# A batched matmul fed from HBM: loads and stores on one queue, and a hardware loop in the middle

## The chip, the cores and the metric

The kernel runs on one core of a Trainium2 chip. The time is device microseconds of that core; the kernel before has a median of 531.79 us over 14 runs (530.21 to 534.66). The profile is of one execution, which took 531.62 us, and from its first to its last instruction it spans 529.5 us.

## The reference

There are 8 x 16 = 128 independent products of a 256 x 512 matrix with a 512 x 384 matrix, in float32:

```python
b1, b2, m, k, n = 8, 16, 256, 512, 384
x = randn(b1, b2, m, k);  weight = randn(b1, b2, k, n)      # float32
out = np.matmul(x, weight)                                   # (8, 16, 256, 384) float32
```

The inputs are 67.1 MB of x and 100.7 MB of weight, the output is 50.3 MB: 218.1 MB cross HBM once.

## The kernel before, in words

The batch is worked off in pairs of products. For a pair, x comes in as one tile of 128 partitions by 2048 numbers (1 MB, `load_x`, L60), and each of the two weights as one tile of 128 by 1536 (768 KB, `load_w`, L67). VectorE casts the x tile to bfloat16 (L77), TensorE transposes it in sixteen 128 x 128 pieces into PSUM (L82), VectorE copies those back to SBUF (L86), and VectorE casts the two weights (L110). TensorE then multiplies: 32 matmuls for a pair (L124), each with 64 columns of stationary x and 384 columns of weight, the two products of the pair side by side in the two halves of PSUM's partitions. ScalarE copies each of the two PSUM tiles to SBUF (L131), and one DMA of 768 KB stores the pair's result (L95). The last pair is taken as two groups of one product each (`groups`, L41), with full 128-column matmuls and two stores of 384 KB.

All loads are issued from SP, all stores from ACT; these are two DMA queues. The whole batch is unrolled: each engine has one straight list of instructions. The order within an engine's list is made by the framework's scheduler from the order of the program. `LAG = 3` (L43) asks for stores three groups late; in the built program each store nevertheless stands on ACT right behind the two copies of its own pair. Tiles come from pools, which reuse buffers in turn: 3 x tiles, 6 float32 weight tiles, so three pairs of loads can be in SBUF; 6 output tiles. Besides the wait for a free buffer, a DMA waits for the DMA eight places before it on the semaphore that both share: there are eight such semaphores, over both queues together, so about eight transfers, two pairs' worth of loads and stores, are in flight.

Of the kernel before, what the change touches and what calls it, by code (L numbers as in the profile page):

```python
# [1 line left out]

# [5 lines left out]


@with_exitstack
def kernel(
    ctx: ExitStack,
    tc: tile.TileContext,
    x: bass.AP,
    weight: bass.AP,
    out: bass.AP,
):
    nc = tc.nc
    P = 128  # L20

    b1, b2, M, K = x.shape
    _, _, _, N = weight.shape
    B = b1 * b2
    KO = K // P

    x_rows = x.rearrange("b1 b2 m k -> (b1 b2 m) k")
    o_rows = out.rearrange("b1 b2 m n -> (b1 b2 m) n")
    w_flat = weight.rearrange("b1 b2 k n -> (b1 b2) k n")

    fp32 = mybir.dt.float32
    bf16 = mybir.dt.bfloat16

    GX = 2
    CX = P // GX
    R = GX * M // P


    groups = [2] * ((B - GX) // 2) + [1] * GX  # L41

    LAG = 3  # L43

    const = ctx.enter_context(tc.tile_pool(name="const", bufs=1))
    x_pool = ctx.enter_context(tc.tile_pool(name="x_pool", bufs=3))
    xb_pool = ctx.enter_context(tc.tile_pool(name="xb_pool", bufs=2))
    xt_pool = ctx.enter_context(tc.tile_pool(name="xt_pool", bufs=2))
    w_pool = ctx.enter_context(tc.tile_pool(name="w_pool", bufs=6))
    wb_pool = ctx.enter_context(tc.tile_pool(name="wb_pool", bufs=4))  # L50
    out_pool = ctx.enter_context(tc.tile_pool(name="out_pool", bufs=LAG + 3))
    psum_t = ctx.enter_context(tc.tile_pool(name="psum_t", bufs=2, space=bass.MemoryType.PSUM))
    psum_o = ctx.enter_context(tc.tile_pool(name="psum_o", bufs=3, space=bass.MemoryType.PSUM))

    identity = const.tile([P, P], bf16)
    make_identity(nc, identity)

    def load_x(b):
        x_sb = x_pool.tile([P, R, K], fp32, name="x_sb")
        nc.sync.dma_start(  # L60
            x_sb[:], x_rows[b * M : (b + GX) * M].rearrange("(p r) k -> p r k", r=R)
        )
        return x_sb

    def load_w(b):
        w_sb = w_pool.tile([P, KO, N], fp32, name="w_sb")
        nc.sync.dma_start(w_sb[:], w_flat[b].rearrange("(kp ko) n -> kp ko n", ko=KO))  # L67
        return w_sb

    def transpose_x(x_sb, RG):  # L70


        H = R // RG
        x_bf = xb_pool.tile([P, R, K], bf16, name="x_bf")
        x_t = xt_pool.tile([P, RG, KO, P, H], bf16, name="x_t")
        for r0 in range(0, R, 4):
            nc.vector.tensor_copy(out=x_bf[:, r0 : r0 + 4], in_=x_sb[:, r0 : r0 + 4])  # L77
            for r in range(r0, r0 + 4, 2):
                pt = psum_t.tile([P, 2, KO, P], bf16, name="pt")
                for rr in range(2):  # L80
                    for ko in range(KO):
                        nc.tensor.transpose(  # L82
                            pt[:, rr, ko, :], x_bf[:, r + rr, ko::KO], identity
                        )
                j = r % RG
                nc.vector.tensor_copy(  # L86
                    out=x_t[:, j : j + 2, :, :, r // RG], in_=pt[:]
                )
        return x_t

    waiting = []

    def store():
        dram, out_sb = waiting.pop(0)
        nc.scalar.dma_start(out=dram, in_=out_sb)  # L95

    b = 0
    for n, G in enumerate(groups):
        last = n == len(groups) - 1
        C = P // G  # L100
        RG = G * M // P
        if b % GX == 0:
            x_sb = load_x(b)
        w_sb = [load_w(b + i) for i in range(G)]
        if b % GX == 0:
            x_t = transpose_x(x_sb, RG)
        w_bf = []
        for i in range(G):
            t = wb_pool.tile([P, KO, N], bf16, name="w_bf")
            nc.vector.tensor_copy(out=t[:], in_=w_sb[i][:])  # L110
            w_bf.append(t)
        if last:
            while waiting:
                store()

        out_full = out_pool.tile([P, 2 * M // P, N], fp32, name="out_sb")
        out_sb = out_full[:, :RG]
        for r in range(0, RG, 2):
            po = psum_o.tile([P, 2, 512], fp32, name="po")
            for rr in range(2):  # L120
                for ko in range(KO):
                    for i in range(G):
                        c0 = (b % GX + i) * CX
                        nc.tensor.matmul(  # L124
                            po[i * C : (i + 1) * C, rr, :N],
                            x_t[:, r + rr, ko, c0 : c0 + CX, :],
                            w_bf[i][:, ko, :],
                            start=(ko == 0),
                            stop=(ko == KO - 1),
                        )  # L130
            nc.scalar.copy(out=out_sb[:, r : r + 2, :], in_=po[:, :, :N])  # L131
        waiting.append(
            (
                o_rows[b * M : (b + G) * M].rearrange("(p r) n -> p r n", r=RG),
                out_sb,
            )
        )
        if len(waiting) > LAG or last:
            store()
        b += G  # L140


# [1 line left out]
_INS = ['x', 'weight']  # L144
_OUTS = [((8, 16, 256, 384), 'float32')]


# [23 lines left out]
```

## Time and profile before

| | before |
|---|---|
| median of 14 runs | 531.79 us |
| the profiled execution, its time | 531.62 us |
| its span, first to last instruction | 529.5 us |
| TensorE matmuls, busy | 344.1 us (65%) |
| VectorE, busy | 277.8 us (52%) |
| ScalarE, busy | 103.8 us (20%) |
| DMA queue of the loads: bytes, share of the 16 DMA engines | 167.78 MB, 76.3% |
| DMA queue of the stores | 50.34 MB, 22.9% |
| instruction fetch of one engine's list: packets, bytes | 24, 0.39 MB |
| mean granted TensorE clock | 0.857 |

Times on the page are microseconds unless marked ns. "PE" is TensorE, "PEld" its weight loads, "DVE" VectorE, "ACT" ScalarE, "SPq" and "ACTq" the instruction sequencers that issue DMAs. A share of DMA near 1.00 in a stretch means that all 16 DMA engines had a packet under way all the time; it can pass 1 a little, since records of successive packets overlap by a few ns. In a row of groups, what stands behind the second bar is the engine's idle time just before those instructions and what ended it. L numbers are lines of the kernel.

### The profile page before, as it was taken

The page shows a single profiled execution, that of the slowest core. Times are in us where ns is not written, and L with a number is a line of the kernel's source. Part 1 is how long each engine was busy: PE and PEld are TensorE (multiplying, and loading weights), DVE is VectorE, ACT ScalarE, POOL GpSimd, SP SyncE. Part 2 cuts the span into 40 slices and gives each one's busy share as a digit, 9 for nine tenths or more (in the row PEclk, how much of TensorE's full clock was granted, in tenths as well). Part 3 has the DMA queues.
Part 4 walks back from the last instruction along what each step waited for, and adds up shares of the span by engine and source line. Part 5 has one row for each costly group of instructions (what it writes and reads, how often), then busy time and mean ns, then how long its engine had stood idle before and what let it go on. Part 6 is the DMA issues. An engine that isn't in the chain of part 4 may idle for free.

```text
span 529.5 us, 7363 instructions
## 1 busy us (share of the span) xinstructions
PE 344.1 (65%) x3056; PEld 235.0 (44%) x3056; DVE 277.8 (52%) x320; ACT 103.8 (20%) x129; POOL 0.7 (0%) x6
## 2 busy tenths in 40 slices
PE   4576674675765857646758567576585685765854
PEld 2354453453543535434435345354353454543532
DVE  4555555545546454655554554554645645465454
ACT  1221221211212212112122121121121211212212
POOL 0000000000000000000000000000000000000000
PEclk9988789979788796898697986978979869689798
DMA  8999999999999999999999999999999999999994
GB/s 346 398 424 422 425 420 422 426 419 421 425 420 424 420 422 425 421 423 423 420 424 423 421 422 423 422 423 424 420 422 423 421 424 422 421 422 424 420 401 166
DMA packets 37041, 218.59 MB, mean 413 GB/s; under 512 B 4112, under 2 KB 4112, under 8 KB 28816
## 3 DMA queue, kind: packets, MB, share of 16 engines
q1 hardware_dynamic: 27648, 167.78, 76.3%
q10 hardware_dynamic: 9360, 50.34, 22.9%
q8 instruction: 24, 0.39, 0.3%
q14 instruction: 9, 0.07, 0.0%
HBM read 167.77 MB, written 50.33 MB: 412 GB/s over the span
## 4 chain that ended last, share of the span: by engine, by line
DMA 83%; PE 9%; DVE 5%; issue 1%; SPq 1%; DVEq 0%; ACT 0%
DMA w_sb<-in_weight_dram 46%; DMA x_sb<-in_x_dram 37%; PE po L124 8%; DVE w_bf L110 3%; DVE x_t L86 2%; PE pt L82 1%; SPq L67 0%; DVEq L166 0%; DVE x_bf L77 0%; SPq L60 0%; ACT out_sb L131 0%; DVEq L110 0%; DVEq L77 0%
## 5 line engine op out<-in xcount | busy, mean ns | idle before, releaser
L124 PE MATMUL po<-w_bf,x_t 128*64 128x384 bf16 (+1 forms) x2032 | 276.5, 407 | 165.8 <-DVE w_bf L110 165.0
L124 PEld LDWEIGHTS <-x_t 128*64 128x64 bf16 (+1 forms) x2032 | 174.6, 135 | 252.3 <-DVE w_bf L110 126.7
L131 ACT COPY out_sb<-po 128x768 f32<-128x768 f32 x128 | 102.6, 801 | 421.6 <-PE po L124 421.6
L77 DVE CAST x_bf<-x_sb 128x2048 bf16<-128x2048 f32 x64 | 78.5, 1227 | 135.7 <-DMA x_sb<-in_x_dram 135.7
L110 DVE CAST w_bf<-w_sb 128x1536 bf16<-128x1536 f32 x128 | 119.8, 954 | 28.4 <-DMA w_sb<-in_weight_dram 27.6
L86 DVE COPY x_t<-pt 128x1024 bf16<-128x1024 bf16 x128 | 83.6, 695 | 81.5 <-PE pt L82 81.5
L82 PE MATMUL pt<-identity,x_bf 128*128 128x128 bf16 x1024 | 70.5, 223 | 15.4 <-DVE x_bf L77 15.2
L82 PEld LDWEIGHTS <-x_bf 128*128 128x128 bf16 x1024 | 60.4, 115 | 37.6 <-DVE x_bf L77 28.9
L131 ACT ACT_TABLE_LOAD x1 | 1.3, 1283 | 0.7 <-PEq L155 0.7
masks.py:199 POOL TENSOR_SCALAR_AFFINE_SELECT identity<-identity 128x128 bf16<-128x128 bf16 x1 | 0.3, 294 | 0.1
masks.py:197 POOL MEMSET identity<- 128x128 bf16 x1 | 0.2, 206 | 0.3 <-POOLq L155 0.3
L155 POOL MEMSET const-bfloat16-1.0<- 128x1 bf16 x1 | 0.1, 102 | 0.0
L155 POOL MEMSET const-uint8-127<- 128x1 uint8 x1 | 0.1, 102 | 0.0
L155 POOL MEMSET const-float32-0.0<- 128x1 f32 x1 | 0.1, 99 | 0.2 <-issue 0.2
L155 POOL MEMSET const-float32-1.0<- 128x1 f32 x1 | 0.1, 99 | 0.0
## 6 DMA issues: line engine op xcount, KB each, us to landing
w_sb<-in_weight_dram SPq DMA_DIRECT2D x128, 768.0 KB, 16.1
x_sb<-in_x_dram SPq DMA_DIRECT2D x64, 1024.0 KB, 16.0
out_dram<-out_sb ACTq DMA_DIRECT2D x63, 768.0 KB, 8.3
out_dram<-out_sb ACTq DMA_DIRECT2D x2, 384.0 KB, 2.3
```

The source lines that it names most:

```text
L77: nc.vector.tensor_copy(out=x_bf[:, r0 : r0 + 4], in_=x_sb[:, r0 : r0 + 4])
L82: nc.tensor.transpose(pt[:, rr, ko, :], x_bf[:, r + rr, ko::KO], identity)
L86: nc.vector.tensor_copy(out=x_t[:, j : j + 2, :, :, r // RG], in_=pt[:])
L110: nc.vector.tensor_copy(out=t[:], in_=w_sb[i][:])
L124: nc.tensor.matmul(po[i * C : (i + 1) * C, rr, :N], x_t[:, r + rr, ko, c0 : c0 + CX, :], w_bf[i][:, ko, :], start=(ko == 0), stop=(ko == K ...
L131: nc.scalar.copy(out=out_sb[:, r : r + 2, :], in_=po[:, :, :N])
L155: nc = _bacc.Bacc("TRN2", target_bir_lowering=False, num_devices=1)
```

## The change

Four things are done together.

1. The stores move from ACT to SP, and SP issues everything in the order in which the program says it: for pair s the two weight loads, the x load, and then the store of pair s-4. The weights now come before x, except in the last pair, where x still comes first and the four stores still owed follow its loads.
2. Buffers are persistent and named, not taken from pools: 4 x tiles, 8 float32 weight tiles and 8 output tiles (four pairs of loads, eight pairs of results); two PSUM tiles for results in place of three, four for transposes in place of two.
3. The first eight pairs and the last eight stay unrolled. The 48 between run in a hardware loop of six iterations with eight pairs each. The loads' and stores' addresses are worked out in registers, and the waits inside compare semaphores with counts in registers, so that no barrier stands between iterations.
4. The built program shows what happens at the loop's ends. Nothing waits on the way in. At the exit SP waits until every DMA of the loop has landed and VectorE, ScalarE and TensorE have finished the loop's last pair; then all engines meet at a barrier, and only then SP issues the next load. The stores of the loop's last four pairs are issued after the exit, each behind the loads of a later pair.

What each engine computes is unchanged: the same casts, transposes, matmuls and copies, in nearly the same order.

```diff
-    groups = [2] * ((B - GX) // 2) + [1] * GX
-    LAG = 3
+    U = 8
+    LAG = 4
...
-    x_pool = ctx.enter_context(tc.tile_pool(name="x_pool", bufs=3))
-    w_pool = ctx.enter_context(tc.tile_pool(name="w_pool", bufs=6))
-    out_pool = ctx.enter_context(tc.tile_pool(name="out_pool", bufs=LAG + 3))
-    psum_t = ctx.enter_context(tc.tile_pool(name="psum_t", bufs=2, space=bass.MemoryType.PSUM))
-    psum_o = ctx.enter_context(tc.tile_pool(name="psum_o", bufs=3, space=bass.MemoryType.PSUM))
+    x_sb = [pool.tile([P, R, K], fp32, name=f"x_sb{s}") for s in range(4)]
+    w_sb = [pool.tile([P, KO, N], fp32, name=f"w_sb{s}") for s in range(8)]
+    w_bf = [pool.tile([P, KO, N], bf16, name=f"w_bf{s}") for s in range(4)]
+    out_sb = [pool.tile([P, R, N], fp32, name=f"out_sb{s}") for s in range(8)]
+    pt = [psum.tile([P, 2, KO, P], bf16, name=f"pt{s}") for s in range(4)]
+    po = [psum.tile([P, 2, 512], fp32, name=f"po{s}") for s in range(2)]
...
-    def store():
-        dram, out_sb = waiting.pop(0)
-        nc.scalar.dma_start(out=dram, in_=out_sb)
+    def store(b, s, g=G):
+        nc.sync.dma_start(
+            out=o_rows[bass.ds(b * M, g * M)].rearrange("(p r) n -> p r n", r=g * M // P),
+            in_=out_sb[s % 8][:, : g * M // P],
+        )
...
+    def pair(b, s, lagged):
+        load_w(b, 2 * s)
+        load_w(b + 1, 2 * s + 1)
+        load_x(b, s)
+        for i in range(G):
+            cast_w(2 * s + i)
+        product(transpose_x(s, R), G, 0, [2 * s, 2 * s + 1], s, 0)
+        if lagged:
+            store(b - G * LAG, s - LAG)
+
+    for s in range(U):
+        pair(G * s, s, s >= LAG)
+    with tc.For_i(G * U, B - G * U, G * U, iteration_sync="reg_based") as b:
+        for s in range(U):
+            pair(b + G * s, U + s, True)
+    b = B - G * U
+    for s in range(U - 1):
+        pair(b + G * s, s, True)
+
+    s = U - 1
+    b += G * s
+    load_x(b, s)
+    load_w(b, 2 * s)
+    load_w(b + 1, 2 * s + 1)
+    for k in range(LAG, 0, -1):
+        store(b - G * k, s - k)
+    xt = transpose_x(s, M // P)
+    for i in range(G):
+        cast_w(2 * s + i)
+        product(xt, 1, i, [2 * s + i], s + i, i)
+        store(b + i, s + i, 1)
```

More of the change, by code (lines that the diff above doesn't have):

```diff
@@ L27 @@
     x_rows = x.rearrange("b1 b2 m k -> (b1 b2 m) k")
+    w_rows = weight.rearrange("b1 b2 k n -> (b1 b2 k) n")
     o_rows = out.rearrange("b1 b2 m n -> (b1 b2 m) n")
-    w_flat = weight.rearrange("b1 b2 k n -> (b1 b2) k n")
     fp32 = mybir.dt.float32
     bf16 = mybir.dt.bfloat16
-    GX = 2
-    CX = P // GX
-    R = GX * M // P
-    groups = [2] * ((B - GX) // 2) + [1] * GX
-    LAG = 3
-    const = ctx.enter_context(tc.tile_pool(name="const", bufs=1))
-    x_pool = ctx.enter_context(tc.tile_pool(name="x_pool", bufs=3))
@@ L47 @@
-    xb_pool = ctx.enter_context(tc.tile_pool(name="xb_pool", bufs=2))
-    xt_pool = ctx.enter_context(tc.tile_pool(name="xt_pool", bufs=2))
-    w_pool = ctx.enter_context(tc.tile_pool(name="w_pool", bufs=6))
-    wb_pool = ctx.enter_context(tc.tile_pool(name="wb_pool", bufs=4))
-    out_pool = ctx.enter_context(tc.tile_pool(name="out_pool", bufs=LAG + 3))
-    psum_t = ctx.enter_context(tc.tile_pool(name="psum_t", bufs=2, space=bass.MemoryType.PSUM))
-    psum_o = ctx.enter_context(tc.tile_pool(name="psum_o", bufs=3, space=bass.MemoryType.PSUM))
@@ L55 @@
-    identity = const.tile([P, P], bf16)
-    make_identity(nc, identity)
-    def load_x(b):
-        x_sb = x_pool.tile([P, R, K], fp32, name="x_sb")
+    G = 2
+    C = P // G
+    R = G * M // P
+    PAIRS = B // G
+    U = 8
+    LAG = 4
+    pool = ctx.enter_context(tc.tile_pool(name="sb", bufs=1))
+    psum = ctx.enter_context(tc.tile_pool(name="ps", bufs=1, space=bass.MemoryType.PSUM))
+    identity = pool.tile([P, P], bf16, name="identity")
+    make_identity(nc, identity)
+    x_sb = [pool.tile([P, R, K], fp32, name=f"x_sb{s}") for s in range(4)]
@@ new lines @@
+    x_bf = [pool.tile([P, R, K], bf16, name=f"x_bf{s}") for s in range(2)]
+    x_t = [pool.tile([P, R, KO, P], bf16, name=f"x_t{s}") for s in range(2)]
+    w_sb = [pool.tile([P, KO, N], fp32, name=f"w_sb{s}") for s in range(8)]
[3 more added lines that the diff above has]
+    po = [psum.tile([P, 2, 512], fp32, name=f"po{s}") for s in range(2)]
@@ L60, in load_x @@
+    def load_x(b, s):
         nc.sync.dma_start(
-            x_sb[:], x_rows[b * M : (b + GX) * M].rearrange("(p r) k -> p r k", r=R)
-        )
[L63 to L70, printed above, removed]
-        H = R // RG
[L74 to L89, printed above, removed]
@@ L91 @@
-    waiting = []
-    def store():
-        dram, out_sb = waiting.pop(0)
[L95 to L119, printed above, removed]
+            x_sb[s % 4][:],
@@ new lines, in load_x, with load_w, transpose_x @@
+            x_rows[bass.ds(b * M, G * M)].rearrange("(p r) k -> p r k", r=R),
+        )
+    def load_w(b, s):
+        nc.sync.dma_start(
+            w_sb[s % 8][:],
+            w_rows[bass.ds(b * K, K)].rearrange("(p ko) n -> p ko n", ko=KO),
+        )
+    def store(b, s, g=G):
+        nc.sync.dma_start(
+            out=o_rows[bass.ds(b * M, g * M)].rearrange("(p r) n -> p r n", r=g * M // P),
+            in_=out_sb[s % 8][:, : g * M // P],
+        )
+    def transpose_x(s, RG):
+        H = R // RG
+        xt = x_t[s % 2].rearrange("k r ko c -> k (r ko c)").rearrange(
+            "k (j ko c h) -> k j ko c h", j=RG, ko=KO, c=P, h=H
+        )
+        nc.vector.tensor_copy(out=x_bf[s % 2][:], in_=x_sb[s % 4][:])
+        for r in range(0, R, 2):
+            t = pt[(2 * s + r // 2) % 4]
@@ L120, with cast_w @@
             for rr in range(2):
                 for ko in range(KO):
-                    for i in range(G):
-                        c0 = (b % GX + i) * CX
+                    nc.tensor.transpose(
+                        t[:, rr, ko, :], x_bf[s % 2][:, r + rr, ko::KO], identity
+                    )
+            j = r % RG
+            nc.vector.tensor_copy(out=xt[:, j : j + 2, :, :, r // RG], in_=t[:])
+        return xt
+    def cast_w(s):
+        nc.vector.tensor_copy(out=w_bf[s % 4][:], in_=w_sb[s % 8][:])
@@ L124, with product @@
+    def product(xt, g, i0, ws, o, n):
+        RG = g * M // P
+        for r in range(0, RG, 2):
+            p = po[(n + r // 2) % 2]
+            for rr in range(2):
+                for ko in range(KO):
+                    for i in range(g):
+                        rows = slice(i * (P // g), (i + 1) * (P // g))
                         nc.tensor.matmul(
-                            po[i * C : (i + 1) * C, rr, :N],
-                            x_t[:, r + rr, ko, c0 : c0 + CX, :],
-                            w_bf[i][:, ko, :],
+                            p[rows, rr, :N],
+                            xt[:, r + rr, ko, (i0 + i) * C : (i0 + i + 1) * C, :],
+                            w_bf[ws[i] % 4][:, ko, :],
@@ L130 @@
                         )
[L131 to L140, printed above, removed]
+            nc.scalar.copy(out=out_sb[o % 8][:, r : r + 2, :], in_=p[:, :, :N])
+    def pair(b, s, lagged):
[27 more added lines that the diff above has]
+        store(b + i, s + i, 1)
 _INS = ['x', 'weight']
```

## The prediction

> **What bounds the kernel now.** I read the page's DMA part first, then the busy time of stretches, then the DMA queue's own waits, then the end in order of time. From the page:
>
> ```profile
> PE 344.1 (65%) x3056; PEld 235.0 (44%) x3056; DVE 277.8 (52%) x320; ACT 103.8 (20%) x129; POOL 0.7 (0%) x6
> ...
> q1 hardware_dynamic: 27648, 167.78, 76.3%
> q10 hardware_dynamic: 9360, 50.34, 22.9%
> q8 instruction: 24, 0.39, 0.3%
> ...
> DMA 83%; PE 9%; DVE 5%; issue 1%; SPq 1%; DVEq 0%; ACT 0%
> ```
>
> The two queues take 76.3 + 22.9 = 99.2% of sixteen DMA engines; the busiest compute engine stands at 65%. The stretches (columns: PE, weight loads, DVE, ACT, POOL with counts, then clock, DMA share, GB/s) say when:
>
> ```profile
> 0.00:2.00 2.00, 0.00 (x0) 0.00 (x0) 0.00 (x0) 1.27 (x1) 0.70 (x6) 1.00 0.27 33
> 2.00:4.00 2.00, 0.00 (x0) 0.00 (x0) 0.00 (x0) 0.01 (x1) 0.00 (x0) 1.00 0.74 295
> ...
> 300.00:320.00 20.00, 12.62 (x108) 8.55 (x110) 10.05 (x12) 3.20 (x4) 0.00 (x0) 0.82 1.02 422
> ...
> 514.00:516.00 2.00, 1.85 (x14) 1.40 (x15) 0.09 (x1) 0.00 (x0) 0.00 (x0) 0.57 0.70 295
> 516.00:518.00 2.00, 2.00 (x18) 1.54 (x15) 0.77 (x1) 0.80 (x1) 0.00 (x0) 0.57 0.60 250
> 518.00:520.00 2.00, 1.60 (x22) 1.09 (x18) 1.26 (x2) 0.80 (x1) 0.00 (x0) 1.00 0.22 88
> ...
> 526.00:528.00 2.00, 0.00 (x0) 0.00 (x0) 0.00 (x0) 0.17 (x1) 0.00 (x0) 0.98 0.84 335
> ```
>
> From 4 to 514 us the DMA engines are full, at 421 to 423 GB/s in every stretch of 20 us between 40 and 500. Only the ends have slack. What SP waits for is not data but a place:
>
> ```profile
> SPq L67 <- DMA w_sb<-in_weight_dram: 255.0, 123, 4.0
> SPq L60 <- DMA x_sb<-in_x_dram: 172.3, 61, 4.6
> ```
>
> That is 427 us of waiting for earlier transfers to land (one of the eight in flight), and about 6 us for VectorE (3.0 + 2.9). So loads are always queued ahead. The end, in order of time:
>
> ```profile
> 517.23 1.23 DVE L77 CAST x_bf<-x_sb 128x2048 bf16<-128x2048 f32 x1 [3.13 <-DMA x_sb<-in_x_dram]
> ...
> 521.56 1.81 DVE L110 CAST w_bf<-w_sb 128x1536 bf16<-128x1536 f32 x2
> 522.55 2.39 PEld L124 LDWEIGHTS <-x_t 128*128 128x128 bf16 x16 [3.11 <-DVE w_bf L110]
> ...
> 524.89 0.34 ACTq L95 DMA_DIRECT2D out_dram<-out_sb  x1
> ...
> 526.20 0.34 ACTq L95 DMA_DIRECT2D out_dram<-out_sb  x1
> ```
>
> The share falls to 0.70, 0.60, 0.22 while loads are still landing: some of the 16 engines have finished and others are late (the last weight packet ends near 520.5). From 514 on, with 353, 46 and 54 GB/s in the stretches left out and 5 in the last, 2 x (295+250+88+353+46+54+335+5) KB = 2.85 MB move in 15.5 us, where 6.8 us would do: 8.7 us are idle.
>
> [...] both queues together make 99.2%, and the loads-only stretch from 4 to 16 us runs at 415 to 441 GB/s, as the mixed ones do. [...]
>
> **The change, part by part.**
>
> *Stores on SP, one order: 0 in the middle.* An issue costs SP 0.33 us; four per pair are 1.3 us of the 3.41 MB / 422 = 8.1 us that a pair takes. The address arithmetic and the register waits come on top; the trace has none, so I bound them by nothing and by another 0.5 us each, 3.3 us per pair, still under 8.1. Behind a store on SP stand the next pair's loads. The store of pair s-4 waits for ScalarE; that pair's loads landed two pairs (16 us) before, and landing to second copy takes some 9 us, so it finds its data ready. If not, 13 us of queued transfers cover it.
>
> *Deeper buffers, weights first: 0.* The limit is eight in flight, and it stays. TensorE's and VectorE's work per pair (344.1/64 = 5.4 and 277.8/64 = 4.3 us) fits in 8.1.
>
> *Back-edges: 0, five of them.* TensorE's loop body is some 796 instructions, three blocks; its packets may be fetched anew in each iteration, and a stall of one packet's length (about 1 us) or several is covered by 2.7 us of slack per pair on TensorE and 13 us of queue on SP. Without that cover it would be 5 x 1 to 4 = 5 to 20 us. Extra fetches load the DMA engines: some 6 more packets of 1 to 1.4 us over 16 engines, 0.5 us.
>
> *End: a gain.* Five pairs' stores (3.93 MB, 9.3 us) remain behind the last loads, where before it was two. They cover the last pair's compute, which from the last weight landing takes about 4 us up to the last store's issue (0.96 cast, half of 2.77 matmul, 0.80 copy, waits). So the end is DMA-bound.
>
> *Exit: the loss.* The DMA engines empty once. In the loop's last pair x lands last, at T, with one store behind it in the queue (0.786 MB, 1.9 us). Durations are from the timeline near 305 us: landing to cast 0.5; cast 1.23; wait and transposes until the first copy 0.7; copy 0.65; 32 matmuls 3.3 (full clock) to 5.5, I take 4.2; last copy with wait 0.9. ScalarE ends at T + 8.2. Barrier: 0.6, estimated from the 1.3 us between the last store packet (near 528.2) and the span's end, which hold a landing and more than one barrier. SP's first issue at 0.74 has its first packet near 2.4: 1.65. Packets flow at T + 10.45, after 8.5 us of idleness. Bounds: 6.5 (full clock, no barrier cost, copy overlapped) and 11 (low clock, and a fetch when the loop branch falls through).
>
> *The sum, on the span.* Start: 2(1-33/422) + 2(1-295/422) = 2.4. A dip at 16 to 20 us (364 and 298 GB/s): 0.9, kept. Up to the exit 56 pairs of loads (2.621 MB each) and 52 stores: 187.7 MB / 422.3 = 444.4. The slowest engine is late at the exit: before, the end loses (1-0.70)+(1-0.60)+(1-0.22), times 2, = 3.0 us to this over the whole run; I take 2. Exit 8.5. After it 30.4 MB / 422.3 = 72.0, slowest engine 1.5. Last packet to span end 1.3, fetches 0.5. Total 2.4 + 0.9 + 444.4 + 2 + 8.5 + 72.0 + 1.5 + 1.3 + 0.5 = 533.5, against 529.5. The profiled execution took 2.1 more than its span, and the median lies 0.2 above it: 533.5 + 2.3 = 535.8, I say 536.0, slower by 0.8%.
>
> **Rivals.** 0.2% (1.06 us) is about what a measurement of this kernel can tell from no change.
>
> *Uneven engines and fetches go away; ends faster.* If the loop's instructions stay in place, fetches fall from 24 packets to about 9 and the engines stay level. That removes the 2 + 1.5 of lateness, the 0.5, and 15 x 1.4/16 = 1.3, in all 5.3: 528.2 + 2.3 = 530.5. It decides only from 5.3 us on, since 536.0 - 530.7 must be made up. For it: [...] packets of instructions stand between data packets. [...] 0.11.
>
> *Exit and end cancel: no change.* Exit at 6.5 and half of the lateness gone: 536.0 - 2.0 - 1.8 = 532.2. 0.11.
>
> *The loop's own cost shows.* Back-edges or SP's register work leave fewer than eight in flight, or the exit takes 11 with a late fetch. Five edges at 1 us and exit 11: 536.0 + 5 + 2.5 = 543.5. Against: 13 us of queue. 0.12.
>
> *Forecast: 536.0*, own range 533 to 539. 0.66.
>
> **How the numbers follow.** The likeliest gives 536.0. The range takes in the no-change case, the exit's upper bound and part of the loop's cost: 531.3 to 542, leaving out the faster case and the worst edges. Faster 0.11; same 0.09 (most of the cancelling case); slower 0.80.
>
> **What would show it.** DMA share 1.0 at 422 GB/s through the loop and across back-edges; one hole of about 8 us near 450 us, with ScalarE's last copy and a barrier in it; a tail without the 8.7 us of idleness, last loads landing near 522; SP's waits still on landed transfers, not on ScalarE. Wrong, if holes recur every eight pairs (65 us), if the hole is under 5 or over 11 us, or if the rate inside the loop is not 422.

## The result, and the profile after

The changed kernel takes 542.21 us (median of 10 runs, 541.2 to 543.62), against 531.82 us for the kernel before in the same comparison: 1.0186 times as long, with a 95% interval of 1.0166 to 1.0206. The forecast was 536.0, with a range up to 542.0. The direction was right, the size was not: 10.4 us were lost where some 4 were foreseen.

The profiled execution took 542.08 us and spans 540.3. Its page, whose second line is the mean rate in 40 slices of 13.5 us:

```profile
DMA  8999699999999999999999999999999995799998
GB/s 352 418 410 421 250 379 424 423 423 422 425 423 424 425 423 424 422 424 424 423 423 424 424 424 424 425 424 423 424 424 424 425 424 233 234 425 423 421 424 329
...
q1 hardware_dynamic: 37008, 218.12, 97.6%
q8 instruction: 9, 0.15, 0.1%
```

All data now go through one queue. In the loop, from slice seven on, the rate is 422 to 425 GB/s, and no stretch of 20 us between 80 and 440 us, back-edges among them, is under 422. There are two holes, not one: slice five (54 to 68 us), where the loop begins, and slices 34 and 35 (446 to 473 us), where it ends. And the instruction packets of q8 are 9, where they were 24. In the packet records, which list every transfer with its start and size, each has 16384 bytes, one comes at 113 us and the next at 463. I take them for TensorE's: its 2 x 3056 matmuls and weight loads share the 24 packets at some 64 bytes each, and the page counts no more than 320 instructions on any other engine.

The hole at the loop's start, in stretches of 2 us (last two columns: share of the DMA engines, GB/s):

```profile
58.00:60.00 2.00, 1.30 (x16) 0.67 (x12) 0.96 (x1) 1.46 (x2) 0.00 (x0) 1.00 0.83 345
60.00:62.00 2.00, 0.00 (x0) 0.00 (x0) 1.07 (x1) 0.14 (x1) 0.00 (x0) 1.00 0.15 62
62.00:64.00 2.00, 1.45 (x20) 1.18 (x22) 1.27 (x3) 0.00 (x0) 0.00 (x0) 0.98 0.05 11
64.00:66.00 2.00, 2.00 (x16) 1.15 (x14) 0.17 (x1) 0.00 (x0) 0.00 (x0) 0.50 0.72 230
66.00:68.00 2.00, 2.00 (x18) 1.09 (x14) 0.00 (x0) 0.80 (x1) 0.00 (x0) 0.67 0.71 227
```

and at its end:

```profile
452.00:454.00 2.00, 0.00 (x0) 0.00 (x0) 0.57 (x1) 0.79 (x1) 0.00 (x0) 1.00 0.56 236
454.00:456.00 2.00, 1.08 (x16) 0.93 (x16) 1.24 (x2) 0.00 (x0) 0.00 (x0) 1.00 0.05 22
...
460.00:462.00 2.00, 0.64 (x8) 0.21 (x4) 0.00 (x0) 0.80 (x1) 0.00 (x0) 1.00 0.00 0
462.00:464.00 2.00, 0.00 (x0) 0.00 (x0) 0.00 (x0) 0.00 (x0) 0.00 (x0) 0.82 0.41 91
```

I price a hole as the bytes that 424 GB/s would have moved more: each stretch of 2 us at r GB/s loses 2 (1 - r/424). From 58 to 74 us that gives 7.2 us, from 452 to 466 us 10.5, and from 468 to 472, where 247 and 287 GB/s flow though the DMA engines are busy (shares of 1.04 and 0.91), 1.5 more. The same sum is used for every kernel below.

What SP waited for between 44 and 72 us:

```profile
SPq L67 <- DVEq L130: 14.8, 1, 14.8
SPq L73 <- ACTq L130: 2.3, 1, 2.3
```

L130 is the line of the loop. SP's first load of the loop waited 14.8 us for VectorE's sequencer, and its first store 2.3 us for ScalarE's, each to come to the loop itself. The instructions in order of time show it (start, duration):

```profile
46.70 0.34 SPq L73 DMA_DIRECT2D out_dram<-out_sb  x1
...
60.92 1.23 DVE L85 CAST x_bf<-x_sb 128x2048 bf16<-128x2048 f32 x1 [1.50 <-DMA x_sb<-in_x_dram]
...
62.88 1.29 DVE L94 COPY x_t<-pt 128x1024 bf16<-128x1024 bf16 x2 [0.73 <-PE pt L90]
63.51 1.61 SPq L67 DMA_DIRECT2D w_sb<-in_weight_dram  x2
...
68.17 0.80 ACT L116 COPY out_sb<-po 128x768 f32<-128x768 f32 x1 [1.16 <-PE po L109]
68.33 0.36 SPq L73 DMA_DIRECT2D out_dram<-out_sb  x1
```

SP has issued everything ahead of the loop by 47 us, two pairs before VectorE. Its next issue comes at 63.51, when VectorE has begun the last copy of pair 7, the last pair before the loop. Meanwhile the two pairs in flight land, and at 60 us the transfers stand idle. The first store follows ScalarE's last copy of pair 7 in the same way.

The reason stands in the built program. Inside the loop SP compares counters (semaphores) that belong to the loop, one for each engine, with counts in registers. The program has each engine give its own counter a starting value as the last thing before it enters the loop, so until VectorE has got there the load waits, although the last cast from the buffer that it wants, one of pair 4's, had ended by 35.02 us. The instruction records show it: SP's wait on VectorE's counter begins at 48.65 us, VectorE raises that counter at 63.35 and branches into the loop at 63.71, and the wait ends at 63.40; the wait on ScalarE's counter begins at 65.93, ScalarE raises it at 68.18, and the wait ends at 68.22. "Nothing waits on the way in", as I described the change above, is wrong.

The exit:

```profile
453.43 1.23 DVE L85 CAST x_bf<-x_sb 128x2048 bf16<-128x2048 f32 x1 [1.49 <-DMA x_sb<-in_x_dram]
...
460.80 0.80 ACT L116 COPY out_sb<-po 128x768 f32<-128x768 f32 x1 [1.08 <-PE po L109]
462.22 0.82 SPq L67 DMA_DIRECT2D w_sb<-in_weight_dram  x2
```

This is the chain of the forecast: 8.2 us from the start of the cast to the end of ScalarE's last copy (461.60), where I had 7.7; and 0.62 us from there to SP's first issue, the barrier, where I had 0.6.

### The profile page after: what moved, and what is told of

Its sections match the earlier page's. It is cut to its first block, busy times and chain, and to the rows that moved or that the text cites. A ratio compares the mean times of both kernels' runs of the same rounds, so it can differ in the third digit from the quotient of the medians.

```text
span 540.3 us, 8649 instructions
## 1 busy us (share of the span) xinstructions
PE 322.0 (60%) x3056; PEld 211.7 (39%) x3056; DVE 285.0 (53%) x320; ACT 103.6 (19%) x129; POOL 0.7 (0%) x6
## 5 line engine op out<-in xcount | busy, mean ns | idle before, releaser
L109 PE MATMUL po<-w_bf,x_t 128*64 128x384 bf16 (+1 forms) x2032 | 235.7, 398 | 17.2 <-DVE x_t L94 14.0
L90 PE MATMUL pt<-identity,x_bf 128*128 128x128 bf16 x1024 | 87.8, 252 | 196.8 <-DVE x_bf L85 196.8
L109 PEld LDWEIGHTS <-x_t 128*64 128x64 bf16 (+1 forms) x2032 | 136.9, 134 | 103.8 <-DVE x_t L94 22.6
L98 DVE CAST w_bf<-w_sb 128x1536 bf16<-128x1536 f32 x128 | 122.4, 958 | 88.6 <-DMA w_sb<-in_weight_dram 82.8
L90 PEld LDWEIGHTS <-x_bf 128*128 128x128 bf16 x1024 | 74.8, 125 | 220.1 <-DVE x_bf L85 219.8
L94 DVE COPY x_t<-pt 128x1024 bf16<-128x1024 bf16 x128 | 86.0, 697 | 61.5 <-PE pt L90 42.2
```

The source lines that it names most:

```text
L90: nc.tensor.transpose(t[:, rr, ko, :], x_bf[s % 2][:, r + rr, ko::KO], identity)
L94: nc.vector.tensor_copy(out=xt[:, j : j + 2, :, :, r // RG], in_=t[:])
L98: nc.vector.tensor_copy(out=w_bf[s % 4][:], in_=w_sb[s % 8][:])
L109: nc.tensor.matmul(p[rows, rr, :N], xt[:, r + rr, ko, (i0 + i) * C : (i0 + i + 1) * C, :], w_bf[ws[i] % 4][:, ko, :], start=(ko == 0), sto ...
```

## The experiments

Two theories of the loss. **Ends:** the loop costs time at its two ends alone, at the entry because SP waits for the engines behind it to enter, at the exit because SP waits for the last pair's compute and a barrier. **Order or fixed prices:** the one queue and its order cost the time, or going in and out of a loop stops the engines for a fixed time of its own. In what follows "the changed kernel" is the one above, with its single loop.

### The loop written out

```diff
-    with tc.For_i(G * U, B - G * U, G * U, iteration_sync="reg_based") as b:
+    for b in range(G * U, B - G * U, G * U):
         for s in range(U):
             pair(b + G * s, U + s, True)
```

> The changed kernel with its hardware loop written out: the same order on SP, the same lag of four, the same named buffers, one straight list per engine. Theory (the loop's two ends cost the time: 7.2 us lost near 60 us at the entry, about 12 us near 455 us at the exit): both holes vanish, the rate falls back from 424 to 422 GB/s since TensorE's instructions are fetched all the way again, and the later stores fill the end: span about 526, median about 528, that is 0.7% faster than the kernel before. Rival (the one queue or the order of weights before x costs the time, the loop's ends only show it): slower than the kernel before, 535 or more, with holes that recur.

Measured: 525.75 us, 0.9882 (0.9842 to 0.9922) of the kernel before. Both holes are gone; the same stretches as above:

```profile
58.00:66.00 8.00, 3.79 (x40) 2.33 (x36) 4.44 (x5) 1.02 (x2) 0.00 (x0) 0.87 1.02 423
452.00:464.00 12.00, 7.57 (x77) 4.85 (x78) 7.09 (x9) 2.36 (x3) 0.00 (x0) 0.86 1.02 426
```

The one queue, the order and the buffers are no loss: without the loop they are 1.2% faster than before, and 2 us faster than I expected. The loop alone costs 542.21 - 525.75 = 16.5 us. The holes at its ends are 7.2 + 10.5 + 1.5 = 19.2 us. Two things give some of it back. From 100 to 440 us, by the packet records, data move at 423.8 GB/s in the loop and at 422.3 in the written-out kernel, which is 1.4 us over the 163.6 MB of the 48 pairs; the instruction packets' own bytes are 0.9 of these 1.5 GB/s, and what the rest comes from was not tried. And the end loses 3.0 us (from 520 us on) where the written-out kernel's loses 4.4 (from 504 on). That leaves 19.2 - 1.4 - 1.4 = 16.4, all but 0.1 of the difference.

### The stores back on ACT, without the loop

```diff
-        nc.sync.dma_start(
+        nc.scalar.dma_start(
             out=o_rows[bass.ds(b * M, g * M)].rearrange("(p r) n -> p r n", r=g * M // P),
```

on top of the written-out kernel. The scheduler puts each store right behind its own pair's copies again.

> The changed kernel without its loop, and with the stores back on ACT, each behind the two copies of its own pair. It tells what the one queue and the lag of four are worth alone. Theory (the lag keeps stores for the end, where the transfers stand idle otherwise): about 531.5, as the kernel before, some 3 us above the unrolled one with stores on SP. Rival (the queue that a store is issued on makes no difference, since a transfer waits its turn either way): equal to the unrolled one within 1 us.

Measured: 531.66 us, 0.9993 (0.9979 to 1.0007): the kernel before. So the order of weights and x, four pairs of buffers in place of three, and the division of PSUM are worth nothing together, and the 5.9 us (I had expected some 3) come from the stores. Where, the last stretches say; first this kernel, then the written-out one with stores on SP:

```profile
518.00:520.00 2.00, 2.00 (x28) 1.25 (x23) 1.42 (x2) 0.93 (x2) 0.00 (x0) 1.00 0.22 85
520.00:522.00 2.00, 0.84 (x16) 0.68 (x13) 1.57 (x2) 0.68 (x1) 0.00 (x0) 1.00 0.27 111
522.00:524.00 2.00, 1.04 (x7) 0.66 (x8) 1.74 (x2) 0.00 (x0) 0.00 (x0) 1.00 0.73 295
524.00:526.00 2.00, 1.73 (x11) 0.83 (x9) 0.00 (x0) 1.03 (x2) 0.00 (x0) 1.00 0.00 0
```

```profile
514.00:516.00 2.00, 0.00 (x0) 0.00 (x0) 2.00 (x3) 0.00 (x0) 0.00 (x0) 1.00 0.99 401
516.00:518.00 2.00, 1.51 (x10) 0.93 (x11) 1.30 (x2) 0.00 (x0) 0.00 (x0) 1.00 0.65 270
518.00:520.00 2.00, 1.26 (x8) 0.55 (x6) 0.00 (x0) 1.45 (x2) 0.00 (x0) 1.00 0.55 224
520.00:522.00 2.00, 0.00 (x0) 0.00 (x0) 0.00 (x0) 0.14 (x1) 0.00 (x0) 0.83 0.86 344
```

While the last pair is computed, the first has little or nothing to move, and the second moves the stores kept back. From 510 us on this kernel loses 9.3 us, and the one with stores on SP 4.4 from 504 on: 4.9 us of the difference. The rest is in the middle: from 100 to 440 us data move at 421.3 GB/s here and in the kernel before, and at 422.3 with the stores on SP, which is 1.2 us over 218.1 MB. Whether that small part comes from the queue or from where the stores stand was not tried.

### Stores two and six groups behind, without the loop

```diff
-    LAG = 4
+    LAG = 2
```

and the same with 6.

> The loop written out, stores two groups behind their loads in place of four. Theory (each store kept back for the end is worth its 1.86 us of transfer there): three stores behind the last loads in place of five, 525.75 + 3.7 = 529.5, unless SP's wait for ScalarE lets the queue run dry in the middle, then more. Rival (the gain came from the one queue): 526 within 1 us.

> The loop written out, stores six groups behind. Theory: two more stores at the end, of which only what is idle there can be filled: from 512 us on the unrolled kernel loses about 4.6 us, some 2 of it after the last transfer, so 523 to 524. Rival (the end is bound by the last pair's compute alone): 525.75 within 0.5 us.

Measured: 530.26 (0.9971, 0.9957 to 0.9985) and 525.13 us (0.9883, 0.9858 to 0.9908). With two it is 4.5 us above the lag of four, where two stores' transfers are 3.7, and all of this on the one queue: it is mainly the stores kept for the end that count, not the queue. SP then waits 344.5 us in total for ScalarE, in front of each store, yet the rate in the middle holds (no stretch of 2 us between 30 and 470 us is under 400 GB/s): SP's waits are hidden there behind the transfers that are queued. Six brought 0.6 us by the medians, not the 2 that I expected, and nothing by the ratios to the kernel before, which are 0.9883 and 0.9882. From 514 us on the rates are 392, 332, 272 and 151 GB/s, at DMA shares of 0.95, 0.80, 0.66 and 0.38: I read this as some of the 16 engines having finished their share and others not, and more stores did not mend it. Lags of four and six are the fastest kernels of this study.

### Loads two pairs ahead, with the loop

```diff
-    def pair(b, s, lagged):
-        load_w(b, 2 * s)
-        load_w(b + 1, 2 * s + 1)
-        load_x(b, s)
+    AHEAD = 2
+
+    def pair(b, s, lagged, ahead=True):
+        if ahead:
+            loads(b + G * AHEAD, s + AHEAD)
...
+    for s in range(AHEAD):
+        loads(G * s, s)
...
```

(`loads` issues a pair's two weights and then its x.)

> The changed kernel with its loop, but each pair's loads stand two pairs ahead of its compute in the program's order, so SP has the loads of two more pairs queued before it meets the loop's entry, and at the exit two pairs' loads follow the last x of the loop. Theory (at the entry SP's first load waits until VectorE has gone into the loop, at the exit for the last pair's compute): the hole at the entry vanishes, the one at the exit shrinks from about 10.5 to about 4 us; rate in the loop 424 GB/s; span about 527, median 529. Rival (going in and coming out stop all engines for a fixed time, for instance to fetch instructions): both holes stay, median within 2 us of 542.

Measured: 530.22 us, 0.9966 (0.9953 to 0.998). From 58 to 66 us the rate is 420 GB/s, and among SP's waits between 40 and 72 us there is none for VectorE's or ScalarE's sequencer any more. At the exit:

```profile
458.00:460.00 2.00, 0.00 (x0) 0.00 (x0) 0.00 (x0) 0.00 (x0) 0.00 (x0) 0.50 0.41 170
460.00:462.00 2.00, 0.00 (x0) 0.00 (x0) 0.00 (x0) 0.00 (x0) 0.00 (x0) 0.50 0.08 34
462.00:464.00 2.00, 0.00 (x0) 0.00 (x0) 1.61 (x2) 0.00 (x0) 0.00 (x0) 0.50 0.40 60
464.00:466.00 2.00, 0.59 (x6) 0.59 (x7) 2.00 (x3) 0.00 (x0) 0.00 (x0) 0.50 0.92 369
```

5.0 us are left of 10.5, and 1.3 from 468 to 472. ScalarE's last copy ended at 451.97, long before; what is left is the landing of the last transfers, which fall to 170 and 34 GB/s, the barrier, and the way from SP's issue (462.33) to the first packets. Both ends answer to where the loads stand, so neither is a fixed price of this size. For the 5.0 us that stay a fixed part is not ruled out.

### Loads one pair ahead

The same kernel with `AHEAD = 1`.

> The loop with loads one pair ahead in place of two. One pair's transfers are 8.1 us. Theory: at the entry SP waits some 14.8 us in the changed kernel and 7.2 us of it show, so one more pair queued covers it nearly all (under 1 us shows); at the exit a whole pair's transfers follow the last x of the loop and end about when ScalarE does (8.1 against 8.7 us), so a hole of about 5 us, as with two pairs ahead: 530 to 531. Rival (it takes two pairs to cover an end): half of the gain of two pairs, about 536.

Measured: 529.84 us, 0.9963 (0.9952 to 0.9974). The entry loses nothing, the exit 5.0 us and 1.5 after it: one pair's transfers do as much as two at either end. Loads issued earlier also put each store one pair further behind them, but the end of the kernel loses 3.3 us here and 3.0 in the changed kernel, so the gain is not made there.

### Less work behind the last landing

```diff
+        if s % U == U - 1:
+            load_x(b, s)
+            load_w(b, 2 * s)
+            load_w(b + 1, 2 * s + 1)
+            xt = transpose_x(s, R)
+            for i in range(G):
+                cast_w(2 * s + i)
+        else:
...
```

in the changed kernel's `pair`: only the last pair before the loop and the last of each iteration take x first.

> The changed kernel, but in the last pair before the loop and the last pair of each iteration x is loaded and transposed before the weights are cast, so that less work stands behind the last transfer at both ends of the loop. Theory (the entry's hole lasts until VectorE has begun the last work of the pair before the loop, the exit's until ScalarE has ended the loop's last pair): behind the last landing VectorE has one cast to begin in place of cast, wait and two copies (2.6 us earlier at the entry), and at the exit about 6.4 in place of 8.7 us: some 5 us less than the changed kernel, about 537. Rival (the holes are fixed prices of going in and coming out): 542, within 1 us.

Measured: 538.82 us, 1.0142 (1.0116 to 1.0168): 3.4 us less than the changed kernel by the medians, 2.3 by the ratios, where 5 were expected and a fixed price would have left all. SP's waits at the entry:

```profile
SPq L67 <- DVEq L139: 12.3, 1, 12.3
SPq L73 <- ACTq L139: 2.3, 1, 2.3
```

L139 is the loop in this kernel. The wait for VectorE is 14.8 - 12.3 = 2.5 us shorter, as worked out (2.6), and the hole there 4.1 us in place of 7.2. At the exit the hole is 8.8 in place of 10.5: 1.7 less, not 2.3. Together that is 4.8 us in the profiled execution, which is the fastest of the four and spans 4.3 us less than the changed kernel's. The order of the x and weight transfers of one pair moves the time, through what VectorE and ScalarE have still to do when the queue is empty.

### Two loops of three iterations

```diff
-    with tc.For_i(G * U, B - G * U, G * U, iteration_sync="reg_based") as b:
-        for s in range(U):
-            pair(b + G * s, U + s, True)
+    with tc.For_i(G * U, B // 2, G * U, iteration_sync="reg_based") as b:
+        for s in range(U):
+            pair(b + G * s, U + s, True)
+    with tc.For_i(B // 2, B - G * U, G * U, iteration_sync="reg_based") as b:
+        for s in range(U):
+            pair(b + G * s, U + s, True)
```

> The changed kernel with its loop cut in two loops of three iterations, one right behind the other: one more exit and one more entry, the second entry behind the barrier of the first exit. Theory (an exit empties the transfers for about 12 us; an entry costs only where SP is ahead of VectorE and ScalarE, and behind a barrier it is not): one more hole of 11 to 13 us near 260 us, so 553 to 555. Rival (every entry has a price of its own of about 7 us): 560 to 562.

Measured: 562.22 us, 1.0586 (1.0534 to 1.0637). The total is the rival's, and my own number is missed by 7 or more; but the trace does not put the 20 us where the rival has them. At the joint:

```profile
266.81 0.80 ACT L116 COPY out_sb<-po 128x768 f32<-128x768 f32 x1 [0.45 <-PE po L109]
269.52 0.97 SPq L67 DMA_DIRECT2D w_sb<-in_weight_dram  x2
...
308.62 5.86 SPq L67 DMA_DIRECT2D w_sb<-in_weight_dram  x2
```

From ScalarE's end (267.61) to SP's issue it is 1.9 us, against 0.6 at a plain exit, so an entry behind a barrier costs some 1.3 us, not 7; the joint's hole, from 258 to 280 us, is 13.0 us with its slow patch, at the upper edge of the 11 to 13 of the theory. Beside it, SP takes 5.86 us for two loads near 310 us, in which the profile names 0.4 us of waits; 2.3 us show in the transfers. The end, from 548 us on, loses 6.7 us where the changed kernel's loses 3.0, and the profiled execution takes 3.7 us more than its span where it is 1.8 in the changed kernel. The first entry (6.3 us) and the last exit (9.7 + 1.5) are a little cheaper than in the changed kernel, so 13.0 + 2.3 + 3.7 - 0.9 - 0.8 = 17.3 of the 18.0 us by which the span is longer are placed. Why SP stands still there, and why the end is longer, is not settled. The packet records hold a hint: an instruction packet of 8 KB, not of q8, comes at 312.5 us, while SP stands still (309.1 to 314.1), and four more come between 555.8 and 561.5, where the changed kernel has none after 60 us. Another, at 336.1, goes with no standstill. Whose instructions they are, the records do not say. This run shows a price for exit plus entry of 13 us, and that a second loop had costs which neither theory had.

## Why the prediction was wrong

**What bounds the kernel: right.** In the middle the transfers are full, at 421 to 424 GB/s of data in every kernel with one loop or none, and all but one or two microseconds of each loss or gain lie in stretches in which they are not.

**The failed step: going into the loop cost nothing in my sum.** The term was missing, since I had read the counters' preparation as a formality: it compares with zero and so never waits (VectorE's takes 0.02 us in the trace). I did not ask who else waits on the same counters, and what stands ahead of the starting value on its engine. The entry cost 7.2 us, more than the 6.8 by which the span missed the forecast (540.3 - 533.5). With the slow patch after the exit, the fetches that did not come and the higher rate in the loop, 7.2 + 1.5 - 0.5 - 1.4 = 6.8, which is the whole miss. SP's 13 us of queued transfers, which I had trusted to cover any wait on SP, were there and not enough: the wait is 14.8 us, since SP runs two pairs ahead of VectorE and its wait lasts until VectorE has caught up. From SP's last issue ahead of the loop to its first inside, 16.8 us pass. The difference to 13 is not all that is lost: 4.0 us are lost up to 64 us, 1.8 more up to 68, before the new transfers keep all engines busy, and 1.3 from 68 to 74 in a slow patch.

**Exit: right in kind, near in size.** My estimates were 8.5 us and 2 for the late engines, 10.5 together; the hole is 10.5. The steps inside it hold (8.2 us from cast to last copy for 7.7, barrier 0.62 for 0.6). A slow patch of 1.5 us after the restart was not in it.

**End: right.** 8.7 us of idleness were to be filled by stores kept back, apart from the slowest DMA engine's lateness, an estimate from the shares of 0.70, 0.60 and 0.22 at the end of the kernel before, and the last landing. My sum without its loop terms, 533.5 - 8.5 - 0.5, gives a span of 524.5 for the loop written out (the 2 us that I had estimated for late engines stay in, since without the exit I count that lateness at the end); its span is 523.8.

**Back-edges: right that they cost nothing**, five of them leave no stretch under 422 GB/s for 20 us. **Fetches: wrong in sign.** I took 0.5 us for extra fetches, an estimate made without a trace of a loop. TensorE's loop body is 796 instructions in the built program, at some 64 bytes each a little over three packets of 16384 bytes, the blocks of my prediction, and it was not fetched again in five back-edges: 9 packets in all, none of them between 113 and 463 us. How large a body may be was not tried. The rate in the loop, 423.8 against 422.3 GB/s, is worth 1.4 us in the change's favour, a little over half of it by the instruction packets' own bytes.

**Stores on one queue: right but for a small part.** I had set its worth in the middle at nothing. The runs nearly fit: without the loop the middle runs at 421.3 GB/s with the stores on ACT and at 422.3 with them on SP, and 4.9 of the 5.9 us are in when a store is issued.

**Rivals.** "The loop's own cost shows" was nearest in time (543.5), but for another reason, and so by luck: I had put it on the back-edges and on SP's register work, which cost nothing that can be seen. It had 0.12; a rival "SP is stopped at the entry" did not exist.

## What to carry to other kernels

When a hardware loop like this one, whose waits compare counts in registers, stands inside a kernel whose transfers must never stop, look at its two ends as at two pipeline flushes: ask which engine runs ahead, what it must wait for before its first instruction inside and its first one after, and how many microseconds of transfers are queued at that moment. Here 13 us of queue met a wait of 14.8 at the entry, and the drain at the exit left a hole of 10.5; loads one pair further ahead took off 12.4 us, and the loop written out took off 16.5. Stores kept back by four groups were the cheap part, some 5 us: they fill the end, where this kernel, bound by transfers, otherwise has few to make.

## What the runs showed of the hardware that I had not expected

- A loop body of 796 instructions, some 64 bytes each, ran six times on TensorE without being fetched again (9 instruction packets of 16384 bytes in place of 24), and the data rate was 423.8 GB/s in place of 422.3.
- After each restart of idle transfers at either end of a loop in these traces a patch follows, some 3 to 5 us later, in which the DMA engines are busy but move less: 247 and 287 GB/s from 468 to 472 us in the changed kernel, 298 and 271 with loads two pairs ahead, 255 and 267 from 482 to 486 us behind the last exit of the two loops. It costs 1.3 to 1.5 us at the exits. In these three stretches over three quarters of the bytes are in the packets of x loads (8192 bytes), which take 497 to 524 ns on the mean where from 100 to 440 us they take 312, while the 6144-byte packets keep their 234 to 237 ns. The first start has something like it later, in the kernel before 364 and 298 GB/s at 16 to 20 us, but there it is the 6144-byte packets that are slower (321 ns). The cause was not tried.
